# Feature sums taken from PSUM on VectorE, and split weights of the feed-forward part and of the attention's projections kept in DRAM

## The chip, the cores and the metric

The kernel runs on one core of a Trainium2 chip. The metric is the device time of one execution in microseconds (us). TensorE (PE) multiplies matrices, VectorE (DVE), ScalarE (ACT) and GpSimd (POOL) work on the elements, and SyncE (SP) issues most DMA transfers between DRAM and the on-chip memory SBUF. TensorE writes to a second memory, PSUM, which DVE and ACT read.

## The reference

A decoder layer on 1024 rows with 16 learned rows ahead of them, 1024 features, float32:

```python
u = rmsnorm(h, mix_norm_pre[l])
proj = u @ w_in[l]
q, f_logit, i_in, g_out, v_pool, gate_a, gate_b = jnp.split(proj, cuts, axis=-1)
a = hgrn2(q, f_logit, i_in, g_out, lbs[l], hgrn_out_norm[l])
p = multiscale_pool(v_pool, pool_proj[l], pool_scale[l])
z = (jax.nn.sigmoid(gate_a) * (a @ w_branch_hgrn[l])
     + jax.nn.sigmoid(gate_b) * (p @ w_branch_pool[l]))
h = h + rmsnorm(z @ w_out[l], mix_norm_post[l])
u = rmsnorm(h, ffn_norm_pre[l])
gt = causal_dwconv(u @ ffn_w_gate[l], ffn_conv_w[l], ffn_conv_b[l])
y = (jax.nn.gelu(gt, approximate=True) * (u @ ffn_w_up[l])) @ ffn_w_down[l]
h = h + rmsnorm(y, ffn_norm_post[l])
```

`hgrn2` is a gated linear recurrence over chunks of 64 rows (called the attention part below), `multiscale_pool` takes trailing means over 2, 4, 8 and 16 rows.

## The kernel before

**Precision.** Every operand of a large product is held as two tiles, `hi` (the value rounded to the reduced format fp32r) and `lo` (the rest). ACT makes `hi` with a cast, DVE or POOL makes `lo` with a subtraction; a product is hi x hi + hi x lo + lo x hi, three matmuls. Making the pair is called a split (`wsplit`, line 136 the cast, 137 the subtraction; for the products of the class `Strassen` lines 209 and 210).

**Stages, in order of time.** (1) 0 to about 70 us: the rows are normed, turned by TensorE (`feature_steps`: four transposes into a PSUM bank `pt`, from which ACT makes `uhi` and DVE `ulo`) and multiplied with the v columns of `w_in` (`v_mm`). The first weights are split by `split_wi` (line 447), in turn on DVE and POOL. (2) To about 100 us: two blocks of G (gate of the recurrence), loaded through a `Loader` that splits weights up to three blocks ahead. (3) To about 280 us: the gates a and b, as eight units of `Strassen`. (4) To about 500 us: the attention part, in the order written in `ORDER`: a capital name is a projection with a weight block of 1024 columns, `h0` to `h3` a step of a head. `POOLED` names operations that go to POOL, the splits `wF0`, `wQ0` and others among them. (5) To about 716 us: branch products, and the output projection in three chunks of rows; the rows of each chunk are normed and turned into features of the feed-forward part (`own.add`, `own.norm`, `own.feat`). (6) The feed-forward part: gate and up units of `Strassen` with the convolution on DVE and POOL beside them; then the down product.

**Strassen.** A unit is a product of 1024 x 256 weights with 1024 features x 1028 columns. It is cut into quarters and computed with seven products P1 to P7 in place of eight, each of four steps. Each needs a weight operand and a feature operand. P1, P2 and P4 take quarters of the weights, the others sums of them, which POOL makes (`load_unit`, lines 235 to 238: `swa`, `swb`). The feature operands are the quarters `b11`, `b21`, `b22` and the sums `t1` to `t4`. For the gates these sums are made by `gate_steps`, five generators of three steps each for five stretches of columns; the table `SUMS_AT` says after which tile which generator goes a step on. For the feed-forward part `to_quarters` makes them for each third of a chunk (114 rows, 456 columns in a tile of four feature blocks); the sums are shared between DVE (`combine`, lines 1061, 1063 and 1073) and POOL (`negdiff`, lines 1078 and 1079, and some `lo` tiles of line 334).

**The start of units.** The first `EARLY` = 4 units do P1 and P2 first, in pairs, since these need no sums: P1 goes to a PSUM pair, ACT copies it to SBUF (`p1s`), P2 goes to another pair, and DVE adds both into the result (`put_ffn`, line 1197), which frees the pair. `rest` does the other five. There are four PSUM pairs in this stage (pool `pf`), shared by products and the transposes' `pt` (line 1043). `ahead` splits weights up to four products ahead; on POOL for P1 and P2 of the second pair. Around the end of the output projection the order of PE, ACT, DVE and POOL is the order of the code (`manual_schedule`); each engine and the queue of SP work strictly in their own order.

**Buffers.** Weights rotate through three tiles each of `wraw` (raw), `whi` and `wlo`. `w_out`'s `lo` tiles are already kept in DRAM (`wlos`) by the first chunk for the other two.

```python
    def operand(self, u, p):
        if (u, "first") in self.raws and p in ("P1", "P2"):
            return self.raws[u, "first"][p == "P2"]
        if p in ("P1", "P2", "P4"):
            return self.raws[u, "raw"][("P1", "P2", "P4").index(p)]
        return self.sums[u][("P5", "P6", "P7", "P3").index(p)]
```

Of the kernel before, what the change touches and what calls it, by code (L numbers as in the profile page):

```python
# [14 lines left out]
P = 128  # L15
# [22 lines left out]
SUMS_AT = {5: (1,), 6: (1, 2), 7: (1, 2), 8: (3, 2), 9: (3, 4, 0), 10: (3, 4, 0), 11: (4, 0)}  # L38
# [18 lines left out]
def trunk_kernel(ctx: ExitStack, tc: tile.TileContext, x, meta_tokens, mix_norm_pre,  # L57
# [122 lines left out]
    class Strassen:  # L180
# [7 lines left out]
        def __init__(self, units, run, early, quarters, span, put, whole):  # L188
# [59 lines left out]
        def product(self, u, p, then=None):  # L248

            assert self.seq[self.at] == (u, p)  # L250
            x = pair(p)
# [4 lines left out]
            cuts = [(c0, o0, 512 - o0), (c0 + 512 - o0, 512, n - 512 + o0)][: 1 + (n + o0 > 512)]  # L256
            for k in range(4):
# [3 lines left out]
                for c, o, w in cuts:  # L261
                    pe.matmul(x[:, o : o + w], whi[:, k, :], xh[:, c : c + w], start=(k == 0), stop=False)  # L262
# [26 lines left out]
        def first(self, u):  # L289
# [3 lines left out]
            return (lambda: self.product(u, "P1", lambda x: act.copy(self.p1s[u], x)),  # L293
                    lambda: self.product(u, "P2", lambda x: self.put(u, 0, 0, self.p1s[u], x)))
# [1203 lines left out]
```

## Time and profile before

| | before |
|---|---|
| median of 3 runs | 1397.15 us (1396.82 to 1398.56) |
| the profiled execution | 1396.61 us |
| its span, first to last instruction | 1394.9 us |
| PE / DVE / ACT / POOL busy | 97% / 70% / 41% / 36% |
| mean granted clock of TensorE | 0.990 |
| read from and written to DRAM | 160.84 and 76.05 MB |

The profile shows one execution. L12 is line 12 of the kernel; `out<-in` are tiles by their names in the program, `[3.55 <-DVE wlo L137]` says that the engine stood idle for 3.55 us until DVE's instruction of line 137 had written `wlo`. "PEclk" is the share of the full clock that was granted to TensorE. About 1.7 us of the time lie outside the span.

### The profile page before, as it was taken

The numbers are of one execution on the slowest core, as the hardware profiler recorded it, in microseconds if no ns is written. First come the engines' busy times: TensorE is split into PE (matmuls) and PEld (weight loads), VectorE is DVE, ScalarE is ACT, GpSimd is POOL, SyncE is SP. The second block draws the span as 40 slices with busy tenths as digits, with TensorE's granted clock in tenths as the row PEclk, the third lists the DMA queues.
The fourth block names the chain that finished last, engine by engine and source line by source line (L and its number), as shares of the span: only waits on it lengthen the run. The fifth ranks groups of instructions, "written<-read, shape, count | busy, mean of one in ns | idle before, by whom it ended". The sixth has DMA issues, their size and how long they took to land. (4 is left out here: it accounts for less than half of the span.)

```text
span 1394.9 us, 21573 instructions
## 1 busy us (share of the span) xinstructions
PE 1353.6 (97%) x8405; PEld 1224.6 (88%) x8405; DVE 973.9 (70%) x1381; ACT 565.0 (41%) x945; POOL 508.4 (36%) x379
## 2 busy tenths in 40 slices
PE   8989999999999999999997999999999999999997
PEld 6879999999999899987777788888999988788786
DVE  6694655288975756565579888888887777654557
ACT  5443333356465463126564322222323223543343
POOL 4255331217543611051036565634567552000100
PEclk9999999999999999999998999999999999999999
DMA  6033433321111023589852577665677879966524
GB/s 245 31 100 121 138 104 108 103 73 46 33 33 33 18 76 122 182 265 316 288 172 91 148 218 214 192 173 145 161 166 188 197 194 268 365 231 201 179 71 166
DMA packets 133220, 215.21 MB, mean 154 GB/s; under 512 B 8327, under 2 KB 76523, under 8 KB 133120
## 3 DMA queue, kind: packets, MB, share of 16 engines
q1 hardware_dynamic: 121056, 189.47, 40.2%
q0 software_dynamic: 12064, 24.38, 10.3%
q8 instruction: 66, 1.08, 0.3%
q14 instruction: 34, 0.28, 0.1%
HBM read 160.84 MB, written 76.05 MB: 170 GB/s over the span
## 5 line engine op out<-in xcount | busy, mean ns | idle before, releaser
L262 PE MATMUL P<-v,whi 128*128 128x258 f32 (+2 forms) x528 | 162.6, 322 | 3.5 <-DVE g L1197 2.5
L263 PE MATMUL P<-v,whi 128*128 128x258 f32 (+2 forms) x528 | 161.6, 320 | 0.0
L265 PE MATMUL P<-v,wlo 128*128 128x258 f32 (+2 forms) x528 | 140.8, 321 | 1.1 <-DVE wlo L210 1.1
L137 POOL TENSOR_TENSOR wlo<-wraw,whi 128x1024 fp32r<-128x1024 f32 (+2 forms) x23 | 50.0, 2174 | 183.0 <-ACT whi L136 101.3
L262 PEld LDWEIGHTS P<-v,whi 128*128 128x128 f32 x528 | 100.8, 191 | 11.8 <-DVE g L1197 2.9
L263 PEld LDWEIGHTS P<-v,whi 128*128 128x128 f32 x528 | 100.7, 191 | 7.5
L161 PE MATMUL pd<-rot 128*128 128x512 f32 x272 | 106.0, 390 | 0.3 <-DVE rot L1257 0.3
L162 PE MATMUL pd<-rot 128*128 128x512 f32 x272 | 105.9, 389 | 0.0
L265 PEld LDWEIGHTS P<-v,wlo 128*128 128x128 f32 x528 | 87.9, 190 | 8.8 <-DVE wlo L210 1.3
L136 ACT CAST whi<-wraw 128x1024 fp32r<-128x1024 f32 (+2 forms) x44 | 36.2, 825 | 146.0 <-PE pba L174 31.3
L209 ACT CAST whi<-wraw 128x512 fp32r<-128x512 f32 x90 | 53.0, 617 | 101.8 <-PE P L263 83.9
L1257 DVE TENSOR_TENSOR rot<-yt,rot 128x1024 fp32r<-128x1024 f32 x33 | 41.2, 1250 | 71.0 <-ACT rot L1256 71.0
L210 DVE TENSOR_TENSOR wlo<-wraw,whi 128x512 fp32r<-128x512 f32 x82 | 75.9, 949 | 18.5 <-ACT whi L209 18.5
L1141 POOL TENSOR_TENSOR ys<-y 128x512 f32<-128x512 f32 x22 | 35.2, 1600 | 142.3 <-issue 96.8
L235 POOL TENSOR_TENSOR swa<-wraw,wraw 128x512 f32<-128x512 f32 x30 | 45.5, 1518 | 95.9 <-DMA wraw<-in_w_in_dram 62.4
L160 PE MATMUL pd<-rot 128*128 128x512 f32 x272 | 72.7, 390 | 2.0 <-ACT rot L1256 2.0
L1256 ACT CAST rot<-yt 128x1024 fp32r<-128x1024 f32 x33 | 34.6, 1053 | 90.2 <-PE pd L161 90.2
L209 ACT CAST whi<-swa 128x512 fp32r<-128x512 f32 x60 | 35.9, 619 | 86.8 <-PE P L263 71.6
L1189 DVE SCALAR_TENSOR_TENSOR y<-g,par,y 128x1024 f32<-128x1024 f32 x44 | 65.1, 1479 | 0.7
L160 PEld LDWEIGHTS pd<-rot 128*128 128x128 f32 x272 | 50.9, 188 | 13.5 <-ACT rot L1256 2.9
L210 DVE TENSOR_TENSOR wlo<-swb,whi 128x512 fp32r<-128x512 f32 x60 | 55.6, 932 | 9.7 <-ACT whi L209 9.4
L209 ACT CAST whi<-swb 128x512 fp32r<-128x512 f32 x60 | 35.9, 618 | 62.9 <-PE P L263 62.0
(344 smaller groups left out, 4320.2 us busy)
## 6 DMA issues: line engine op xcount, KB each, us to landing
wraw<-in_w_in_dram SPq DMA_DIRECT2D x36, 512.0 KB
yt<-ysum SPq DMA_DIRECT2D x33, 512.0 KB
wraw<-in_ffn_w_gate_dram SPq DMA_DIRECT2D x26, 512.0 KB
wraw<-in_w_out_dram SPq DMA_DIRECT2D x24, 512.0 KB
wraw<-in_ffn_w_up_dram SPq DMA_DIRECT2D x22, 512.0 KB
wsum<-in_ffn_w_down_dram SPq DMA_DIRECT2D x22, 512.0 KB
ysum<-ys SPq DMA_DIRECT2D x11, 768.0 KB
sa<-sscr SPq DMA_DIRECT2D x16, 513.0 KB
```

The costliest lines, as they stand in the source:

```text
L137: eng.tensor_tensor(lo, raw, rr(hi), ALU.subtract)
L160: pe.matmul(ps, ahi, bhi, start=first, stop=False)
L161: pe.matmul(ps, ahi, blo, start=False, stop=False)
L162: pe.matmul(ps, alo, bhi, start=False, stop=last)
L209: act.copy(hi, src)
L210: (pool_e if 4 <= i < 2 * self.early else dve).tensor_tensor(lo, src, rr(hi), ALU.subtract)
L235: pool_e.tensor_tensor(s1, a21, a22, ALU.add)
L262: pe.matmul(x[:, o : o + w], whi[:, k, :], xh[:, c : c + w], start=(k == 0), stop=False)
L263: pe.matmul(x[:, o : o + w], whi[:, k, :], xl[:, c : c + w], start=False, stop=False)
L265: pe.matmul(x[:, o : o + w], wlo[:, k, :], xh[:, c : c + w], start=False, stop=(k == 3))
L1189: dve.scalar_tensor_tensor(a, g[:, :, j : j + n], cvw[:, j, m : m + 1], a, ALU.mult, ALU.add)
L1257: dve.tensor_tensor(lo, src, rr(hi), ALU.subtract)
```

## The change

1. Ahead of everything else on TensorE stand five idle matmuls (`warm`) into a bank that nobody reads. All splits of `split_wi` are on DVE.
2. In `gate_steps` all of POOL's sums go to DVE. For the last three tiles t1 and t2 are made directly from the transposes' PSUM bank, right behind `ulo` (`more`). `SUMS_AT` is changed accordingly.
3. While the gates are computed, one job behind each half unit (`keep_next`): for the twelve weight blocks of F, Q and PV the split is made and `lo` written to DRAM (`keep_job`); for the first four feed-forward gate units P1's and P2's weights are split and both tiles written (`keep_first`). In the attention part F, Q and PV read `lo` back (`wload`), with no subtraction, and `ORDER` has seven new entries: `w4` (three) and `w5` (four), in each of which one or two weight operands of feed-forward units 0 (gate) and 4 (up) are summed on DVE, split and written to DRAM (`keep_unit`).
4. The first 20 products of the feed-forward part read both tiles from DRAM (`kept`), with no split and no sums. P2 of the first four units adds onto P1's PSUM pair (`onto`), after ACT has copied P1 out; ACT copies the result to the gate tile. The last chunk's feature sums are all on DVE, in pieces (`todo`) with a place of their own each.

```diff
-SUMS_AT = {5: (1,), 6: (1, 2), 7: (1, 2), 8: (3, 2), 9: (3, 4, 0), 10: (3, 4, 0), 11: (4, 0)}
+SUMS_AT = {5: (2,), 6: (2, 1), 8: (3,), 9: (1, 3), 10: (1, 4), 11: (4, 0), 12: (0, 0)}
...
+                if i % 2 == 0 and i // 2 < len(self.kept):
+                    parts_, tags = self.kept[i // 2]
+                    both = [wst.tile([P, 1024], F32R, tag=t, name=nm(t), bufs=NRAW) for t in tags]
+                    for t, src in zip(both, parts_):
+                        self.loaded = nc.sync.dma_start(rr(t), src)
...
-        def product(self, u, p, then=None):
+        def product(self, u, p, onto=None):
-            x = pair(p)
+            x = pair(p) if onto is None else onto
...
-        (pool_e if len(wi) % 2 else dve).tensor_tensor(lo, raw, rr(hi), ALU.subtract)
+        dve.tensor_tensor(lo, raw, rr(hi), ALU.subtract)
...
+    def sums_of(t0):
+        a = slice(t0 - 512, t0 - 512 + P)
+        t1, t2 = t12[a.start] = halves_tmp(P)
+        def more(j, src):
+            if j == 0:
+                dve.tensor_tensor(t1, src, rr(uhi[:, :4, a]), ALU.subtract)
+                dve.tensor_tensor(t1, t1, rr(ulo[:, :4, a]), ALU.subtract)
+            else:
+                dve.tensor_tensor(t2, src, t1, ALU.subtract)
+        return more
...
+    def keep_unit(u, w):
...
+        if u >= EARLY:
+            keep(((u, "P1"), a11), ((u, "P2"), a12))
+            yield
+        keep(((u, "P6"), ((a21, ADD, a22), (None, SUB, a11))), ((u, "P5"), ((a21, ADD, a22),)))
+        yield
+        keep(((u, "P3"), ((a21, ADD, a22), (None, SUB, a11), (a12, SUB, None))), ((u, "P7"), ((a11, SUB, a21),)))
+        yield
+        keep(((u, "P4"), a22))
...
+    def keep_job(kind, i):
+        raw = wraw_tile()
+        nc.sync.dma_start(raw.rearrange("p (k c) -> p k c", k=KD), job(kind, i)[0])
+        hi, lo = (wst.tile([P, 1024], F32R, tag=t, name=nm(t)) for t in ("whi", "wlo"))
+        act.copy(hi, raw)
+        dve.tensor_tensor(lo, raw, rr(hi), ALU.subtract)
+        kept_w[kind, i] = dram.tile([P, 1024], F32, name=f"kept{kind}{i}")
+        owed.append((kept_w[kind, i], rr(lo)))
+    def wload(*key):
...
+        nc.sync.dma_start(rr(lo), kept_w[key])
+        act.copy(hi, raw)
...
+        def first(e):
+            x[e] = ffn.product(e, "P1")
+            keep(e)
+        def second(e):
+            ffn.product(e, "P2", x[e])
+            act.copy(gate_tile(2 * UNITS[e][0])[:, 0], x[e][:, o : o + n])
```

The orders below give, for one engine, line, operation, output and inputs with their buffer numbers, and the tile.

DVE around the splits of G's weights (`L137`), before; `tt` are the gates' sums:

```order
L334 TENSOR_TENSOR t2l_578<-tt_121_638,t2h_576 128x2x128
L334 TENSOR_TENSOR t2l_579<-tt_121_638,t2h_577 128x2x128
L840 TENSOR_TENSOR tt_121_638<-tt_121_638,uhi_86 128x512
L842 TENSOR_TENSOR tt_121_638<-uhi_86,tt_121_638 128x512
L137 TENSOR_TENSOR wlo_721<-wraw_718,whi_720 128x1024
L137 TENSOR_TENSOR wlo_727<-wraw_724,whi_726 128x1024
```

The same place after the change; `L963` to `L967` are the first step of `gate_steps`, `L348` is the old line 334:

```order
L348 TENSOR_TENSOR t4l_628<-tt_64_355,t4h_626 128x2x128
L348 TENSOR_TENSOR t4l_629<-tt_64_355,t4h_627 128x2x128
L963 TENSOR_TENSOR tt_126_678<-ulo_87 128x512
L964 TENSOR_TENSOR tt_126_678<-uhi_86 128x512
L965 TENSOR_TENSOR tt_126_678<-tt_126_678 128x512
L966 TENSOR_TENSOR tt_126_678<-uhi_86,tt_126_678 128x512
L967 TENSOR_TENSOR tt_126_678<-tt_126_678,ulo_87 128x512
L137 TENSOR_TENSOR wlo_741<-wraw_738,whi_740 128x1024
L137 TENSOR_TENSOR wlo_747<-wraw_744,whi_746 128x1024
```

Ahead of the splits now stands the whole first step of one stretch, with the two operations that POOL did; the t1 and t2 of other stretches were made earlier.

DVE at the start of the feed-forward part, before: the last norm, the sum that frees P2's pair (`L1197`), the first third's sums (`tt_1041`, from the ACT copy `tt_1043`), the next release:

```order
L1120 SCALAR_TENSOR_TENSOR un_7222<-m_1008_7133,rstd_7226,g_790_6121 114x1024
L1197 TENSOR_TENSOR g_7254<-p_1015_7146,P_1031_7229 128x514
L1073 TENSOR_TENSOR tt_1041_7281<-tt_1043_7282,v_787_6117 128x456
L1073 TENSOR_TENSOR tt_1041_7281<-tt_1041_7281,v_787_6117 128x456
L1061 TENSOR_TENSOR tt_1041_7281<-tt_1043_7282,tt_1041_7281 128x456
L334 TENSOR_TENSOR t2l_6931<-tt_1041_7281,t2h_6929 128x2x114
L334 TENSOR_TENSOR t2l_6932<-tt_1041_7281,t2h_6930 128x2x114
L1063 TENSOR_TENSOR tt_1043_7282<-tt_1043_7282 128x456
L334 TENSOR_TENSOR v_788_6118<-tt_1041_7281,v_788_6118 128x4x114
L334 TENSOR_TENSOR t3l_6935<-tt_1043_7282,t3h_6933 128x2x114
L334 TENSOR_TENSOR t3l_6936<-tt_1043_7282,t3h_6934 128x2x114
L1197 TENSOR_TENSOR g_7328<-p_1015_7146,P_1044_7303 128x514
```

And after (`tt_1095` the first third's, `tt_1101` the second third's):

```order
L1262 SCALAR_TENSOR_TENSOR un_7455<-m_1074_7377,rstd_7459,g_857_6365 114x1024
L1215 TENSOR_TENSOR tt_1095_7471<-tt_1097_7472,v_854_6361 128x456
L1215 TENSOR_TENSOR tt_1095_7471<-tt_1095_7471,v_854_6361 128x456
L1202 TENSOR_TENSOR tt_1095_7471<-tt_1097_7472,tt_1095_7471 128x456
L348 TENSOR_TENSOR t2l_7175<-tt_1095_7471,t2h_7173 128x2x114
L348 TENSOR_TENSOR t2l_7176<-tt_1095_7471,t2h_7174 128x2x114
L1215 TENSOR_TENSOR tt_1101_7517<-tt_1103_7518,v_854_6361 128x456
L1215 TENSOR_TENSOR tt_1101_7517<-tt_1101_7517,v_854_6361 128x456
L1202 TENSOR_TENSOR tt_1101_7517<-tt_1103_7518,tt_1101_7517 128x456
L348 TENSOR_TENSOR t2l_7175<-tt_1101_7517,t2h_7173 128x2x114
L348 TENSOR_TENSOR t2l_7176<-tt_1101_7517,t2h_7174 128x2x114
```

No sum that frees a pair stands among them any more, t2 of the second third comes ahead of the first third's t1, t3 and t4, and those follow further down.

PE at the same place, before: the last two matmuls of P2 of unit 0, the transposes of the first third, P2 of unit 1:

```order
L265 MATMUL P_1031_7229<-v_787_6117,wlo_7139 128x258
L265 MATMUL P_1031_7229<-v_787_6117,wlo_7139 128x256
L1043 MATMUL pt_7272<-ident,un_7101 128x114 x8
L262 MATMUL P_1044_7303<-v_787_6117,whi_7138 128x258
L263 MATMUL P_1044_7303<-v_787_6117,whi_7138 128x258
```

And after: the last two of P1 of unit 1, the transposes, then P2 of unit 0, which goes to `P_1078`, the pair of its P1:

```order
L275 MATMUL P_1086_7424<-v_854_6361,wraw_7276 128x258
L275 MATMUL P_1086_7424<-v_854_6361,wraw_7276 128x256
L1182 MATMUL pt_7462<-ident,un_7341 128x114 x8
L272 MATMUL P_1078_7382<-v_854_6361,wraw_7336 128x258
L273 MATMUL P_1078_7382<-v_854_6361,wraw_7336 128x258
```

The transposes stand one product earlier, and fewer pairs are in use at once.

More of the change, by code (lines that the diff above doesn't have):

```diff
@@ L356, in norm_rows, with feature_steps @@
         return list(norm_steps(row, rows, gbc))[-1]
-    def feature_steps(un, rows, uhi, ulo, t_at):
+    def feature_steps(un, rows, uhi, ulo, t_at, more=None):
         for j in range(2):
@@ L434, in trunk_kernel, with warm @@
     g1 = slot(D, name="g1")
+    junk_bank = bank("pj")
+    def warm(n):
+        for _ in range(n):
+            pe.matmul(junk_bank[:, :P], onesm, ident, start=True, stop=True)
+    warm(2)
     gps = [bank("pg1") for _ in range(2)]
@@ new lines, in wload @@
+    def wload(*key):
+        raw = wraw_tile()
+        nc.sync.dma_start(raw.rearrange("p (k c) -> p k c", k=KD), job(*key)[0])
+        hi, lo = (wst.tile([P, 1024], F32R, tag=t, name=nm(t)) for t in ("whi", "wlo"))
+        nc.sync.dma_start(rr(lo), kept_w[key])
+        act.copy(hi, raw)
+        return tuple(t.rearrange("p (k c) -> p k c", k=KD) for t in (hi, lo))
+    beside = [lambda o=o_: keep_job(*o) for o_ in order if o_[0] in ("F", "Q", "PV")]
+    beside += [lambda e=e: keep_first(e) for e in range(EARLY)]
@@ L936, in trunk_kernel @@
     gates.finish()
+    pay()
     close_pool("pf")
     open_pool("ps", 8, PSUM)
-    loader = Loader([job(*o_)[:2] + (P, eng("w%s%d" % o_)) for o_ in order if o_[0].isupper()])
+    assert not beside
+    loader = Loader([o_ if o_ in kept_w else job(*o_)[:2] + (P, eng("w%s%d" % o_)) for o_ in order if o_[0].isupper()],
+                    lambda *a: wload(*a) if isinstance(a[0], str) else wsplit(*a))
     def split_z(c, k):
@@ L1273, in trunk_kernel @@
     last, t4s = None, []
+    assert ffn.seq[: len(KEPT)] == KEPT
+    ffn.kept = list(zip(kept, (("wraw", "wraw"), ("wraw", "wlo")) + (("whi", "wlo"),) * len(KEPT)))
     load_rows(0)
@@ L1295, in trunk_kernel @@
                             add_quarters("t2", "t3", "t4")
-                        t4s.append(last.feat(k - 2))
-                    if k > 4 and t4s:
-                        t4s.pop(0)()
+                        *now, late = last.feat(k - 2) or [None]
+                        for f in now:
+                            f()
+                        t4s += [late] * bool(now)
             if c < 2:
```

224 lines of the change are left out of this document (149 added, 75 removed).

## The prediction

> **What bounds the kernel now.** I read the page's busy times first, then the busy times by stretches, then what TensorE waited for.
>
> ```profile
> span 1394.9 us, 21573 instructions
> PE 1353.6 (97%) x8405; PEld 1224.6 (88%) x8405; DVE 973.9 (70%) x1381; ACT 565.0 (41%) x945; POOL 508.4 (36%) x379
> ```
>
> TensorE is busy for 1353.6 of 1394.9 us. The change leaves its number of products as it is, so it can only win back some of the 41.3 us in which TensorE stands still, and the time in which it runs at half its clock. The table by stretches says where these lie. Its columns are the stretch, its length, then busy time (instructions) of PE, PEld, DVE, ACT and POOL, then the granted clock, the DMA share and GB/s.
>
> ```profile
> 20.00:60.00 40.00, 40.00 (x205) 33.16 (x204) 24.51 (x47) 20.46 (x43) 3.57 (x4) 1.00 0.24 78
> 60.00:80.00 20.00, 16.42 (x69) 13.82 (x68) 19.69 (x21) 8.92 (x20) 14.01 (x9) 0.84 0.17 52
> 100.00:120.00 20.00, 17.63 (x148) 17.64 (x149) 4.90 (x15) 8.55 (x22) 11.56 (x11) 1.00 0.33 111
> 130.00:280.00 150.00, 150.00 (x1225) 150.00 (x1225) 74.12 (x98) 50.18 (x85) 41.51 (x28) 1.00 0.36 116
> 340.00:480.00 140.00, 136.18 (x1052) 132.28 (x1051) 112.23 (x234) 76.40 (x122) 67.14 (x31) 0.99 0.11 31
> 640.00:700.00 60.00, 57.70 (x271) 44.05 (x270) 33.53 (x50) 37.05 (x70) 0.00 (x0) 1.00 0.88 306
> 700.00:716.00 16.00, 15.15 (x69) 11.08 (x68) 13.64 (x25) 10.65 (x29) 6.49 (x8) 1.00 0.47 158
> 700.00:720.00 20.00, 18.09 (x91) 13.78 (x90) 17.57 (x31) 14.31 (x37) 6.49 (x8) 1.00 0.45 150
> 720.00:740.00 20.00, 16.68 (x141) 16.25 (x139) 16.95 (x18) 10.02 (x23) 10.78 (x8) 0.98 0.49 152
> 740.00:760.00 20.00, 13.84 (x78) 13.43 (x79) 18.87 (x25) 10.23 (x25) 11.60 (x9) 0.67 0.24 79
> 760.00:780.00 20.00, 18.29 (x115) 15.82 (x114) 17.04 (x18) 6.82 (x13) 18.52 (x18) 1.00 0.35 80
> 780.00:800.00 20.00, 18.25 (x105) 15.84 (x105) 18.50 (x24) 6.11 (x10) 6.29 (x6) 1.00 0.62 182
> ...
> 72.00:82.00 10.00, 6.49 (x27) 6.49 (x28) 9.83 (x9) 3.76 (x9) 7.79 (x5) 0.66 0.44 134
> 740.00:750.00 10.00, 6.39 (x32) 6.39 (x33) 9.41 (x13) 3.41 (x10) 6.96 (x6) 0.52 0.47 157
> 756.00:760.00 4.00, 3.91 (x18) 3.72 (x19) 3.98 (x6) 3.92 (x10) 2.71 (x2) 0.57 0.00 0
> ```
>
> ```profile
> PE pt L1043 <- DVE g L1197: 6.2, 1, 6.2
> PE pg L177 <- DVE wlo L137: 3.6, 1, 3.6
> PE P L262 <- ACT sg L714: 2.7, 1, 2.7
> PE P L262 <- ACT t2h L333: 2.5, 1, 2.5
> ```
>
> These are TensorE's waits (total, times, longest). The five stretches from 700 to 800 us hold 100 - (18.09 + 16.68 + 13.84 + 18.29 + 18.25) = 14.85 us of idle TensorE. A stall also slows what follows: at 740 to 750 us the clock is 0.52, so 6.39 us busy are worth 3.3 and 3.1 are lost; at 756 to 760 us another 3.91 x 0.43 = 1.7. The start of the feed-forward part thus costs 14.85 + 3.1 + 1.7 = 19.6 us, and only 0.85 of it (idle from 700 to 716) belongs to the output projection. The wait for G's weights costs 3.55 us plus 6.49 x 0.34 = 2.2 of lost clock.
>
> **Part 1, the first microseconds.** A row of the groups by line (gates, 130 to 280 us) gives the price of a split of 1024 columns on DVE with little beside it; then rows in order of time (start, duration).
>
> ```profile
> L137 DVE TENSOR_TENSOR wlo<-wraw,whi 128x1024 fp32r<-128x1024 f32 x1 | 1.2, 1226 | 0.2 <-ACT whi L136 0.2
> ...
> 2.44 3.75 PE L437 MATMUL pg<-g1row,ones 1*128 1x512 f32 x4 [2.44 <-DMA g1row<-in_mix_norm_pre_dram]
> 6.62 0.86 DVE L352 SCALAR_TENSOR_TENSOR un<-row,rstd,g 128x512 f32<-128x512 f32 x1
> 7.63 1.09 PE L363 MATMUL pt<-ident,un 128*128 128x128 f32 x4 [1.45 <-POOL mask L495]
> 11.35 3.56 DVE L352 SCALAR_TENSOR_TENSOR un<-row,rstd,g 128x512 f32<-128x512 f32 x2
> 11.70 2.66 POOL L447 TENSOR_TENSOR wlo<-wiraw,whi 128x1024 fp32r<-128x1024 f32 x1 [2.73 <-ACT whi L446]
> 12.08 0.63 PE L160 MATMUL pv<-whi,uhi 128*128 128x512 f32 x1
> ...
> 12.51 0.63 PE L161 MATMUL pv<-wlo,uhi 128*128 128x512 f32 x1
> ...
> 16.04 0.39 PE L161 MATMUL pv<-wlo,uhi 128*128 128x512 f32 x1
> ...
> 16.27 0.39 PE L162 MATMUL pv<-whi,ulo 128*128 128x512 f32 x1
> ```
>
> The two halves of the second norm take 3.56 us beside POOL's weight split; alone one took 0.86, so 1.8 us of stretching goes. In its place DVE has the split to do, 1.23 us, which may come before or after them. I take -1. The first six products start 0.43 us apart (12.08, 12.51) and from 16.04 on 0.23: at full pace they would save 6 x 0.2 = 1.2 us if nothing else held them. Bounds: 0 and -2. The five idle matmuls go ahead of the gain's broadcast, which waits for its DMA until 2.44. Five at the 0.27 us of a transpose are 1.4 us, twice that if each is two passes. The gain is broadcast until 6.19 and its second half copied only after the first norm half (7.48), so about 1.2 us of delay is covered besides the wait for the DMA: cost 0 (at most 0.6). The Trainium skill ("TensorE: Matmul & The Clock Gate", Part 1) holds that the clock is released only after about 3.4 us of sustained work, in free-running windows; by that the idle matmuls, a gap of over 1 us behind them, wake nothing early and the term is -1; were they to wake it, -2. The stretch from 12 to 16 us fits the rule, but says nothing on so short a burst.
>
> **Part 2, the gates' sums and G's weights.**
>
> ```profile
> 71.85 0.68 DVE L840 TENSOR_TENSOR tt<-tt,uhi 128x512 f32<-128x512 f32 x1
> 73.17 4.50 DVE L137 TENSOR_TENSOR wlo<-wraw,whi 128x1024 fp32r<-128x1024 f32 x2
> 75.51 0.94 PE L177 MATMUL pg<-uhi,wlo 128*128 128x342 f32 x2 [3.55 <-DVE wlo L137]
> ```
>
> DVE is busy for 19.69 of the 20 us from 60 to 80. The first split of G's weights starts at 73.17, behind the sums L840 and L842, and two splits take 4.50 us beside POOL's sums where one alone takes 1.23. After the change nothing of POOL's stands beside them, and three tiles' first sums (three operations of 0.68 each, 6.1 us) are made earlier, between the v products, where DVE is busy for 24.51 of 40 us and TensorE for all (20 to 60). Against this the second halves of POOL's sums come to DVE: about two more operations per tile, 1.4 us, and five sums now stand straight ahead of the splits. The splits themselves end 2 us sooner than 4.50, and the queue ahead of them is shorter by the contention of five to ten operations. I take the stall as gone with its lost clock, 3.55 + 2.2, but for 0.3: -5.5. Bounds: 0 (the queue is as late as before) and -5.8. What is late next is the wait of 2.7 us for the change of PSUM pools (L714), which stays.
>
> **Part 3, the weights kept in DRAM.** While the gates are computed, 12 jobs each split 1024 columns and four split two halves of 512: on DVE 12 x 1.23 + 8 x 0.68 = 20 us, on ACT about as much. From 130 to 280 us DVE is busy for 74.12 of 150 us and ACT for 50.18, TensorE for all 150.00: the cover is there. DMA moves 12 x 1 MB + 4 x 1.5 MB more, 120 GB/s on top of 116, and 306 GB/s have been seen (640 to 700). I take +1; with 0.3 us lost at each of 16 jobs it would be +5, and 0 is the other end.
>
> In the attention part the splits of F, Q and PV leave POOL (ten) and DVE (two), and their place is taken by seven pieces w4 and w5, 26 DVE operations of 512 columns, 26 x 0.68 = 17.7 us.
>
> ```profile
> 352.66 3.40 POOL L137 TENSOR_TENSOR wlo<-wraw,whi 128x1024 fp32r<-128x1024 f32 x1
> 353.72 3.44 DVE L626 TENSOR_TENSOR kd<-kd,kk 128x1040 f32<-128x1040 f32 x1
> ```
>
> The DVE operation of 1040 columns took 3.44 us beside POOL's split, 1.23 being the price of 1024 alone. At 1 to 2 us each the ten POOL splits have cost DVE 10 to 20 us, the two DVE splits at least 2.5: relief and new work come out near each other. DVE is busy for 112.23 of the 140 us, and the stretch has 3.8 us of idle TensorE. I take +1, bounds -4 (all that idle) and +6 (a third of the new work uncovered).
>
> **Part 4, the start of the feed-forward part.**
>
> ```profile
> 736.96 1.69 DVE L1063 TENSOR_TENSOR tt<-tt 128x456 f32<-128x456 f32 x1
> ...
> 743.61 1.78 PE L1043 MATMUL pt<-ident,un 114*128 114x114 f32 x8 [6.20 <-DVE g L1197]
> ...
> 747.15 0.70 DVE L334 TENSOR_TENSOR t2l<-tt,t2h 128x228 fp32r<-128x228 f32 x2 [0.45 <-ACT t2h L333]
> 747.77 0.63 DVE L1063 TENSOR_TENSOR tt<-tt 128x456 f32<-128x456 f32 x1
> ```
>
> The wait of 6.20 us: the transposes need the PSUM pair that the gate sum L1197 frees, and this stands on DVE behind the whole of the first third's sums, each slowed by POOL (1.69 us against 0.63 for L1063). After the change P2 is added onto P1's pair and ACT copies it out, so that no release stands behind DVE's sums; the splits of these products and POOL's sums of units 0 and 4 are gone. What DVE then has is eight operations of 456 columns and three pairs of 228 for each third: 3 x (8 x 0.63 + 3 x 0.70) = 21.4 us. TensorE's first eight products are 24 matmuls each, of 0.12 us by the gates (1225 matmuls in 150.00 us), 2.9 us a product, and with the three thirds' transposes (at most 1.5 us each, by the 743.61 row and the next product at half clock) 25 to 27 us. It fits, but in places only just. I went through the new order by hand with these durations. TensorE waits 1.1 us before P2 of unit 2 and 2.45 before P2 of unit 3 (ACT's copy of P1 stands behind casts that wait for DVE), 0.95 before P6 for the last third's t2, and 1.95 in four later places: 6.5 us in place of 19.6 - 0.85 = 18.8, a gain of 12.3. Waits of 2.5 (t2h) and 2.7 us (sg) stand in the list above; behind the first the clock fell to 0.57 and 1.7 us went, behind the second it stayed at 1.00 (100 to 120 us). So I charge 1 us for the wait of 2.45 and take -11. Bounds: -5, if each of those waits is twice as long, and -17, if hardly any comes. The Trainium skill (same page and part) puts the fall of the clock at an idle window of about 3.4 us. By that a wait of 2.45 us would cost no clock, the term would be -12 and the time 1380, inside the forecast's own range; the row at 756 to 760 us speaks against the rule as an exact threshold.
>
> The kept operands, 20 halves of 512 KB or 10.5 MB, have to come within some 60 us, 175 GB/s, where half of that came as raw weights before (150 GB/s from 700 to 740) and 306 were seen: hidden, and if not, the gain of this part shrinks by the same time.
>
> **Sum.** -1 - 5.5 + 1 + 1 - 11 = -15.5. The profiled execution took 1396.61 us, 0.54 under the median of 1397.15: 1396.6 - 15.5 = 1381.1.
>
> **Rivals.**
> - The sums stay the bound at the feed-forward start (DVE busy 17 to 19 of 20 us there speaks for it; that POOL's share is slowing it speaks against): -5 for -11, 1387.
> - All goes better: -17 there, -4 in the attention part, 0 in the gates, 1396.6 - 1 - 5.8 - 4 - 17 = 1369. Against it: the hand reckoning leaves waits.
> - It does not do what it says: DVE reaches G's weights as late as before and the kept operands come so late that TensorE waits as long as it did: terms 0 and 0, 1396.6 - 1 + 1 + 1 = 1397.6. Against it stands the DMA rate above.
> - Slower: the pieces w4 and w5 come where DVE has no room (340 to 480 us), and TensorE waits for all of their 17.7 us, with one more fall of the clock (2.2): +20 in place of +1, 1396.6 - 1 - 5.5 + 1 + 20 - 11 = 1400. It decides once more than 16.5 us of the 17.7 and its after-effects are uncovered. Against it: 27.8 us of free DVE in that stretch, and what POOL's splits no longer cost.
>
> **How the numbers follow.** Forecast (1376 to 1385) 0.53, sums stay the bound 0.20, better 0.12, no effect 0.07, slower 0.08. The range from 1368 to 1394 leaves out the last two and the end of the better case, and takes in the bounds of parts 2 and 4 one at a time (forecast with part 2 at 0: 1386.6; with part 4 at -5: 1387; both, 1392.6). A measurement of this kernel tells about 0.2%, 2.8 us, from no change: faster 0.85, same 0.07, slower 0.08.
>
> **What would show it.** In the profile after: no wait of pg for wlo near 72 us and a clock of 1.00 from 72 to 82; no wait of pt for L1197's successor; TensorE busy over 93 of the 100 us behind the output projection's end, with its waits naming ACT's p1 copies and t2; 150 us of full TensorE in the gates as before; idle time in the attention part near 3.8 us. The forecast is wrong if idle time there grows beyond 10 us, or if products wait for DMA of the kept tiles.

## The result and the profile after

The changed kernel takes 1387.03 us (median of 4 runs, 1386.05 to 1390.67) against 1397.86 of the kernel before beside it: a ratio of 0.9927, interval 0.991 to 0.9945. That is faster by 0.7%, inside the range and above the forecast's own 1376 to 1385. The page's busy times after:

```profile
span 1386.2 us, 21763 instructions
PE 1352.8 (98%) x8415; PEld 1224.7 (88%) x8415; DVE 970.8 (70%) x1436; ACT 578.4 (42%) x961; POOL 419.7 (30%) x320
```

TensorE's work is the same; of the 8.7 us that the span lost, 7.9 are idle time of TensorE. The stages show that this is a difference of large terms. Lengths in us, read from the order in time of each profile, each from the first matmul of a stage to the first of the next (start to the first gate product; gates to the first F product; attention to the first branch product; branch products; output projection). The feed-forward units count to the start of their last matmul, and the down product from there to the start of its own last:

| kernel | start, v, G | gates | attention | branch | output proj. | feed-forward | down |
|---|---|---|---|---|---|---|---|
| before | 102.4 | 160.0 | 250.4 | 94.2 | 109.2 | 458.0 | 213.3 |
| after | 93.8 | 168.0 | 260.0 | 94.8 | 108.4 | 440.3 | 213.2 |
| difference | -8.6 | +8.0 | +9.6 | +0.6 | -0.8 | -17.7 | -0.1 |

Busy times by these stretches, gates, attention and feed-forward units, before (columns as in the prediction):

```profile
102.37:262.35 159.98, 159.98 (x1345) 159.98 (x1346) 78.39 (x106) 54.87 (x95) 54.34 (x38) 1.00 0.36 118
262.35:512.78 250.43, 246.61 (x1837) 240.58 (x1836) 186.90 (x383) 136.63 (x219) 108.93 (x52) 0.99 0.14 42
716.14:1174.16 458.02, 444.01 (x2796) 401.54 (x2795) 383.10 (x455) 143.67 (x247) 254.76 (x194) 0.99 0.67 179
```

and after:

```profile
93.79:261.77 167.98, 162.55 (x1344) 161.96 (x1345) 97.35 (x135) 70.52 (x121) 52.41 (x37) 0.99 0.68 213
261.77:521.76 259.99, 249.55 (x1836) 242.28 (x1835) 196.13 (x407) 144.81 (x233) 89.62 (x43) 0.99 0.32 105
724.92:1165.23 440.31, 438.01 (x2796) 397.29 (x2795) 364.56 (x451) 135.64 (x233) 220.88 (x167) 1.00 0.73 199
```

In the gates TensorE stood still for nothing before and for 5.4 us now, and in the attention part for 10.4 us in place of 3.8, though DVE is busy for only 97 of 168 and 196 of 260 us. In the feed-forward units its idle time fell from 14.0 to 2.3 us. TensorE's longest waits after follow; the wait for G's weights is gone from the list:

```profile
PE ppp L173 <- DVE sc L697: 3.6, 1, 3.6
PE P L272 <- ACT whi L217: 2.8, 1, 2.8
PE P L272 <- ACT p L1473: 1.8, 2, 1.2
PE pj L456 <- POOL ident masks.py:199: 1.6, 1, 1.6
```

**The gates.** Rows in order of time around the wait of 2.8 us for `whi`:

```profile
152.21 0.38 SPq L236 DMA_DIRECT2D wraw<-in_w_in_dram  x1
...
156.75 1.30 POOL L243 TENSOR_TENSOR swa<-wraw,wraw 128x512 f32<-128x512 f32 x1 [11.30 <-DMA wraw<-in_w_in_dram]
...
159.26 1.72 POOL L244 TENSOR_TENSOR swa<-swa,wraw 128x512 f32<-128x512 f32 x1
...
160.98 1.04 ACT L924 CAST whi<-wraw 128x1024 fp32r<-128x1024 f32 x1 [1.74 <-DMA wraw<-in_w_in_dram]
...
161.93 0.61 ACT L217 CAST whi<-swa 128x512 fp32r<-128x512 f32 x1
```

and the second raw load of the same unit (the fourth) before, where the gates start 8.6 us later:

```profile
142.27 0.42 SPq L228 DMA_DIRECT2D wraw<-in_w_in_dram  x1
```

The unit's second raw half is asked for 58.4 us after the gates' first product (152.21 - 93.79) where it was 39.9 before (142.27 - 102.37): its buffer had just been released by a kept job's subtraction (L925). POOL waits for it, its sums are late, and on ACT the cast of the next kept job (L924) stands ahead of the one that TensorE needs, itself waiting for a load. The stall also took clock (0.72):

```profile
162.00:168.00 6.00, 5.40 (x32) 5.40 (x33) 4.29 (x6) 3.26 (x7) 0.33 (x1) 0.72 0.94 270
```

The rest of the 5.4 us are two stalls of 1.3 and 1.4 us, up to 211.45 and 215.93 us. Ahead of the first, a cast on ACT had waited 2.58 us for a raw load; ahead of the second, a subtraction on DVE had waited 3.02 us for the store of a job's `lo`. Between the stalls, with the jobs running, TensorE is never idle:

```profile
118.00:159.50 41.50, 41.50 (x350) 41.50 (x349) 22.91 (x31) 14.63 (x23) 9.89 (x8) 1.00 0.68 210
168.00:209.50 41.50, 41.50 (x350) 41.50 (x349) 27.08 (x33) 18.12 (x28) 12.38 (x8) 1.00 0.75 231
217.00:261.70 44.70, 44.70 (x378) 44.70 (x377) 28.43 (x40) 20.35 (x34) 7.01 (x5) 1.00 0.81 259
```

**The attention part.** DVE and POOL ahead of the wait of 3.6 us (TensorE's last matmul before it starts at 469.62; the kernel before had one of 2.5 us near this place, up to 477.06, so 1.1 us of it are new):

```profile
466.01 2.41 DVE L871 TENSOR_TENSOR wlo<-wlo,wraw 128x512 f32<-128x512 f32 x1
...
467.95 4.56 POOL L776 TENSOR_TENSOR s<-s 128x1037 f32<-128x1037 f32 x2
...
468.74 2.00 DVE L871 TENSOR_TENSOR wlo<-wraw,wlo 128x512 f32<-128x512 f32 x1
...
470.66 2.39 DVE L874 TENSOR_TENSOR wlo<-wlo,whi 128x512 fp32r<-128x512 f32 x1
...
472.98 1.28 DVE L697 COPY_PREDICATED sc<-mbase,sb 128x128 f32<-128x128 uint8 x6
```

L871 and L874 are a piece w5. The copies L697, which free the PSUM banks that the next projection needs, stand behind them, and each operation takes 2.0 to 2.4 us beside POOL's sums instead of 0.68. The Trainium skill ("SBUF — State Buffer", Who interferes with whom) states that a DVE instruction with two inputs in SBUF contends with a GpSimd instruction that reads SBUF; these rows agree.

More of the new idle time lies elsewhere. From 363 to 379 us there are four waits of 0.9 to 1.4 us, 4.3 us in all, among the operations of a piece w4 on DVE (L871 and L874); the kernel before has no wait over 0.7 us there. And at the start of the stage, up to 266.45 us, TensorE waits 1.2 and 1.1 us for the first casts of `wload` (L934).

### The profile page after: what moved, and what is told of

Its sections match the earlier page's. It is cut to its first block, busy times and chain, and to the rows that moved or that the text cites. A ratio compares the mean times of both kernels' runs of the same rounds, so it can differ in the third digit from the quotient of the medians.

```text
span 1386.2 us, 21763 instructions
## 1 busy us (share of the span) xinstructions
PE 1352.8 (98%) x8415; PEld 1224.7 (88%) x8415; DVE 970.8 (70%) x1436; ACT 578.4 (42%) x961; POOL 419.7 (30%) x320
## 5 line engine op out<-in xcount | busy, mean ns | idle before, releaser
L272 PE MATMUL P<-v,whi 128*128 128x258 f32 (+1 forms) x496 | 153.4, 323 | 2.3 <-ACT p L1473 1.8
L273 PE MATMUL P<-v,whi 128*128 128x258 f32 (+1 forms) x496 | 152.3, 321 | 0.0
L275 PE MATMUL P<-v,wlo 128*128 128x256 f32 (+2 forms) x512 | 136.7, 320 | 0.0
L272 PEld LDWEIGHTS P<-v,whi 128*128 128x128 f32 x496 | 93.5, 189 | 10.3 <-ACT p L1473 2.2
L273 PEld LDWEIGHTS P<-v,whi 128*128 128x128 f32 x496 | 93.7, 189 | 7.6
L275 PEld LDWEIGHTS P<-v,wlo 128*128 128x128 f32 x512 | 84.8, 189 | 7.8
L217 ACT CAST whi<-wraw 128x512 fp32r<-128x512 f32 x78 | 46.2, 617 | 95.8 <-PE P L273 79.2
L243 POOL TENSOR_TENSOR swa<-wraw,wraw 128x512 f32<-128x512 f32 x28 | 42.5, 1519 | 117.4 <-DMA wraw<-in_w_in_dram 73.5
L217 ACT CAST whi<-swa 128x512 fp32r<-128x512 f32 x56 | 33.5, 618 | 94.2 <-PE P L273 64.6
L160 PEld LDWEIGHTS pd<-rot 128*128 128x128 f32 x272 | 51.0, 188 | 13.4 <-ACT rot L1399 1.6
L218 DVE TENSOR_TENSOR wlo<-swa,whi 128x512 fp32r<-128x512 f32 x56 | 51.7, 932 | 15.4 <-ACT whi L217 10.4
L161 PEld LDWEIGHTS pd<-rot 128*128 128x128 f32 x272 | 51.1, 188 | 11.3 <-DVE rot L1400 0.7
L162 PEld LDWEIGHTS pd<-rot 128*128 128x128 f32 x272 | 51.1, 188 | 10.6
L272 PE MATMUL P<-t2h,whi 128*128 128x258 f32 (+1 forms) x196 | 57.1, 308 | 2.8 <-ACT whi L217 2.8
```

What stands on the lines that cost most here:

```text
L160: pe.matmul(ps, ahi, bhi, start=first, stop=False)
L161: pe.matmul(ps, ahi, blo, start=False, stop=False)
L162: pe.matmul(ps, alo, bhi, start=False, stop=last)
L217: act.copy(hi, src)
L218: (pool_e if 4 <= i < 2 * self.early else dve).tensor_tensor(lo, src, rr(hi), ALU.subtract)
L243: pool_e.tensor_tensor(s1, a21, a22, ALU.add)
```

## Experiments

Stage lengths of all runs, in us, with the time and the ratio to the kernel before. The lengths are those of one profiled execution each. In the seven runs whose feed-forward part is that of the changed kernel, that column goes from 440.3 to 444.2, so a difference of 3 or 4 us there says little:

| run | gates | attention | branch | output proj. | feed-forward | median | ratio (interval) |
|---|---|---|---|---|---|---|---|
| after | 168.0 | 260.0 | 94.8 | 108.4 | 440.3 | 1387.03 | 0.9927 (0.991 to 0.9945) |
| e_sums | 160.2 | 250.7 | 94.4 | 108.7 | 458.9 | 1388.91 | 0.9947 (0.993 to 0.9964) |
| e_nojobs | 168.2 | 259.1 | 94.9 | 109.3 | 441.1 | 1388.57 | 0.9938 (0.9918 to 0.9958) |
| e_ownraw | 181.6 | 265.2 | 94.9 | 109.9 | 443.9 | 1405.67 | 1.0061 (1.0043 to 1.0078) |
| e_late | 168.4 | 251.9 | 94.2 | 108.6 | 440.4 | 1379.89 | 0.9878 (0.9857 to 0.9899) |
| e_lateall | 160.3 | 250.7 | 106.5 | 114.1 | 444.2 | 1387.70 | 0.9932 (0.991 to 0.9953) |
| e_actstore | 176.1 | 267.4 | 94.8 | 108.7 | 443.4 | 1403.83 | 1.005 (1.0033 to 1.0067) |
| e_nounits | 167.7 | 254.6 | 94.2 | 108.7 | 455.1 | 1394.62 | 0.9987 (0.9975 to 0.9999) |
| e_pool | 168.2 | 261.6 | 94.8 | 108.9 | 440.1 | 1390.94 | 0.9966 (0.9946 to 0.9986) |
| e_late_own3 | 168.7 | 252.9 | 94.8 | 109.2 | 441.8 | 1382.52 | 0.9894 (0.9876 to 0.9911) |
| e_unitsonly | 160.3 | 250.7 | 94.4 | 108.1 | 445.9 | 1375.12 | 0.985 (0.9831 to 0.987) |
| e_jobdma | 160.3 | 250.7 | 95.2 | 108.7 | 446.6 | 1376.21 | 0.9829 (0.9809 to 0.9849) |
| e_jobwork | 160.3 | 250.6 | 95.5 | 108.7 | 447.2 | 1377.55 | 0.9838 (0.9815 to 0.9861) |

**e_sums: part 2 (and the first splits) alone.** The kernel before with:

```diff
+SUMS_AT = {5: (2,), 6: (2, 1), 8: (3,), 9: (1, 3), 10: (1, 4), 11: (4, 0), 12: (0, 0)}
-        pool_e.tensor_tensor(t2, b12l, b11l, ALU.subtract)
+        dve.tensor_tensor(t2, b12l, b11l, ALU.subtract)
...
-        (pool_e if len(wi) % 2 else dve).tensor_tensor(lo, raw, rr(hi), ALU.subtract)
+        dve.tensor_tensor(lo, raw, rr(hi), ALU.subtract)
```

> The kernel before with part 2 and the first weights' splits on DVE alone: nothing is kept in DRAM, no idle matmuls, the feed-forward part as before. Theory: the whole gain between 60 and 102 us comes from this part, so the first gate product starts at about 93.8 us as in the changed kernel (102.4 before), all later stages keep their lengths, and the time is 8 to 9 us under before (ratio about 0.994). Rival: part of that gain needs the rest of the change (fewer POOL operations later, other buffer use); then the first gate product starts later than 97 us and the gain is under 5.5 us.

The first gate product starts at 93.49 us, and all later stages have their old lengths. The gain up to the gates is this part's alone: the theory holds. Alone it makes the kernel 8.0 us faster (1396.91 to 1388.91), where the whole change gains 10.8: parts 3 and 4, which make up most of the code, add some 3 us to it.

**e_nojobs: without the twelve jobs for F, Q and PV.**

```diff
-    beside = [lambda o=o_: keep_job(*o) for o_ in order if o_[0] in ("F", "Q", "PV")]
-    beside += [lambda e=e: keep_first(e) for e in range(EARLY)]
+    beside = [lambda e=e: keep_first(e) for e in range(EARLY)]
```

> The changed kernel without the twelve jobs for F, Q and PV: their splits are made in the attention part on POOL and DVE as before; the four jobs for the first feed-forward products and w4, w5 stay. Theory (the twelve jobs cost the gates 8 us, w4 and w5 cost the attention part its 10): gates 160 to 163 us instead of 168, attention part (first F product to first branch product) 260 us or some more, since POOL's splits come back beside w4 and w5: time 1379 to 1386. Rival (reading lo back and ACT's casts at the head of its queue cost the attention part, not w4 and w5): attention part 250 to 253 us, time 1369 to 1373.

The gates stay at 168.2: my price by the number of jobs fell. Four jobs at the worst place cost as much as sixteen. The rows at the one long stall:

```profile
152.58 1.29 DVE L874 TENSOR_TENSOR wlo<-wraw,whi 128x512 fp32r<-128x512 f32 x2 [3.10 <-DMA kept3l<-wlo]
...
153.90 0.38 SPq L236 DMA_DIRECT2D wraw<-in_w_in_dram  x1
...
159.81 1.26 POOL L243 TENSOR_TENSOR swa<-wraw,wraw 128x512 f32<-128x512 f32 x1 [13.89 <-DMA wraw<-in_w_in_dram]
...
161.10 0.62 ACT L217 CAST whi<-swa 128x512 fp32r<-128x512 f32 x1 [9.36 <-POOL swa L243]
```

The chain is that of the changed kernel: a raw buffer that a job's subtraction (L874, itself behind a wait for an earlier store) frees late, the raw load 60.9 us after the gates' start, POOL's sum, the cast. The stall is 4.9 us long, and the clock behind it is 0.50 from 165 to 168 us and 0.78 to 171. From 165 us on, with no jobs, TensorE is busy all the time. The attention part, which here reads no `lo` back but still has w4 and w5, falls by only 0.9 us, so the theory is right there: the pieces cost 8 to 9 us. The waits at the start of that stage are gone in this run; they come with the reading back.

**e_ownraw: the jobs' raw tiles from another pool.**

```diff
-        raw = wraw_tile()
+        raw = slot(1024, name="kraw")
```

> The changed kernel, but the jobs beside the gates take their raw weights into a buffer of the feature pool, so the three raw buffers serve the gates' units alone. Theory (the gates' 8 us come from the raw buffers' rotation: the next unit's weights are loaded late): gates 160 to 162 us instead of 168, time 1379 to 1382. Rival (the jobs' work on DVE and ACT or their DMA delays the gates): gates 166 to 169 us, time 1385 to 1389.

Slower by 0.6%: the raw buffers alone are not the cause. The gates' products now end 170.3 us after their start, and a wait of 11.1 us follows. What SP waited for from 90 to 280 us in this run says where the jobs pass the wait on (L817 and L819 are the gates' own stores, which wait long without any job, too: 86 us in the kernel before):

```profile
SPq L819 <- ACT sg L815: 42.1, 14, 7.5
SPq L888 <- DVE wlo L925: 25.6, 12, 6.0
SPq L817 <- ACT sg L815: 21.5, 13, 5.3
SPq L888 <- ACT whi L873: 16.5, 5, 4.9
```

The jobs' stores (L888) wait at the head of SP's queue for tiles that are late, with the units' loads behind them.

**e_late: w4 and w5 among the branch products.**

```diff
-F2 w4 h1 c2 h0 Q2 w4 h1 h2 G2 w4 ... F3 w5 ... PV0 w5 ... PV1 w5 ... PV2 w5 ... BB1 BB2 sa2 BB3 h3 BB4
+F2 h1 c2 h0 Q2 h1 h2 G2 ... F3 ... PV0 ... PV1 ... PV2 ... BB1 w4 BB2 sa2 w4 BB3 h3 w4 BB4
-BB5 sa0 sa3 BA0 BA1 BB6 BA2 BB7 BA3 BA4
+BB5 sa0 sa3 w5 BA0 BA1 w5 BB6 BA2 w5 BB7 BA3 w5 BA4
```

> The changed kernel with the seven pieces w4 and w5 moved out of the attention part, to between the branch products BB1 and BA4, where DVE is busy for 80 of 140 us. Theory (the attention part's 10 us are DVE's 26 operations of these pieces ahead of copies that free PSUM): first F product to first branch product 250 to 253 us instead of 260, the branch products 0 to 3 us longer, time 1377 to 1382. Rival (the loads of lo and ACT's casts cost it): that stretch stays at 258 to 261, time 1385 to 1390.

Attention 251.9, branch products 94.2, as the theory has it, and a kernel faster than the one before and the changed one. The same 26 DVE operations cost nothing there, as the row of the branch products shows (DVE 63.54 of 94.17 us, TensorE all of them):

```profile
512.19:606.36 94.17, 94.17 (x592) 92.99 (x591) 63.54 (x102) 35.44 (x53) 13.50 (x9) 1.00 0.71 246
```

**e_lateall: all of the keeping among the branch products.** No jobs for F, Q and PV; `keep_first` there as well, as k0 to k3. Against e_late's order:

```diff
-BB0 h2 ... BB4 BB5 ... BB7 BA3 w5 BA4 BA5
+BB0 k0 h2 ... BB4 k1 BB5 ... BB7 k2 BA3 w5 BA4 k3 BA5
```

> Nothing is kept during the gates and the attention part: no jobs for F, Q and PV (split on POOL and DVE as before), and the four jobs for the first feed-forward products as well as w4 and w5 stand among the branch products BB0 to BA5. Theory (the gates' 8 us and the attention part's 10 are the price of keeping, where it was put): gates 160 to 161 us, first F product to first branch product 250 to 251, branch products 94 to 99 instead of 95, feed-forward part as in the changed kernel: time 1368 to 1375. Rival (the jobs only meet another limit there: DMA or the raw buffers): branch products and output projection 8 us or more longer, time over 1377.

Gates and attention are back at 160.3 and 250.7, but the branch products take 12 us more and the output projection 5: the rival came true. What TensorE waited for longest in that run:

```profile
PE pba L173 <- ACT whi L136: 5.0, 3, 2.5
```

The branch products' own weights now come late: from 500 to 700 us ACT waits 16.1 us, in five waits, for loads of them. On SP's queue the kept stores wait 23.9 us for casts in that time; how much of the delay is theirs, and how much that of the DMA rate (261 GB/s in the branch products, 167 in the changed kernel), is open.

**e_actstore: the jobs' stores on ACT's queue.**

```diff
-        pay()
         if beside:
             beside.pop(0)()
+        pay(nc.scalar)
```

> The changed kernel, but the jobs' stores beside the gates are issued on ACT's queue right behind each job, not on SP's ahead of the next loads. Theory A (SP works in order, and the stores, waiting for DVE's lo and standing behind the gates' own stores, hold up the next unit's loads): gates 160 to 164 us instead of 168, time 1379 to 1384. Theory B (the buffers shared with the jobs set when the loads can start, whatever the queue): gates 166 to 170, time 1385 to 1390.

176.1 us, worse than either theory said. Where ACT has to wait for DVE before it can issue the store, everything behind it waits too. ACT's longest wait from 90 to 270 us (9.9 us in the changed kernel, to 262 us):

```profile
ACT whi L217 <- DVE wlo L925: 21.8, 10, 5.2
```

On SP's part in the loss this run says nothing.

**e_nounits: only the first eight products kept.**

```diff
-    KEPT += [(0, p) for p in Strassen.ORDER[2:]] + [(UP0, p) for p in Strassen.ORDER]
...
         second(0)
+        ffn.load_unit(RUN[0])
         do(0)
...
+        ffn.load_unit(RUN[1])
         ffn.rest(RUN[0], dict(P6=[lambda: do(2, 3)]))
```

> The changed kernel with only the first eight feed-forward products kept; the rest of unit 0 and unit 4 are loaded raw, summed on POOL and split on DVE as before, and w4, w5 are gone. Theory: the attention part is short again (first F product to first branch product 250 to 253), and the feed-forward part's products take 443 to 449 us instead of 440, so half or more of its 18 us come from the first eight products, the PSUM release and the sums' place: time 1380 to 1387. Rival (the kept units 0 and 4 carry that gain): 450 to 458 us, time 1388 to 1396.

The attention part falls to 254.6 with w4 and w5 gone, though not to 250 to 253. What is left lies at its start: TensorE waits 2.7 us for the first casts of `wload`, and the clock falls to 0.61 and 0.53 (264 to 272 us). e_late waits 2.1 us there, with 0.62 and 0.96. So the reading back costs some 1.5 to 4 us. In the feed-forward part the rival came true: 455.1 us, so the kept units 0 and 4 carry 14.8 of the 17.7 us when they are taken away alone. The rows around one of three long waits (3.3, 3.0 and 3.4 us) show how:

```profile
736.77 1.44 POOL L246 TENSOR_TENSOR swb<-wraw,swa 128x512 f32<-128x512 f32 x1
...
736.98 2.38 DVE L1214 TENSOR_TENSOR tt<-tt,v 128x456 f32<-128x456 f32 x2
...
740.14 0.67 ACT L347 CAST t2h<-tt 128x228 fp32r<-128x228 f32 x2 [3.80 <-DVE tt L1201]
...
742.28 0.39 PE L272 MATMUL P<-v,whi 128*128 128x258 f32 x1 [3.26 <-ACT p L1472]
```

Unit 0's weight sums are back on POOL beside DVE's feature sums (1.19 us each against 0.63); ACT's copy of P1 stands behind the cast that waits for them, and P2, which goes to the same pair, waits 3.26 us for the copy.

**e_pool: the last chunk's feature sums shared with POOL again.**

```diff
-        todo.append(own.feat(0, dve))
+        todo.append(own.feat(0))
```

(the same for 1 and 2)

> The changed kernel with the last chunk's b22, t4 and difference sums back on POOL, all else as changed. Theory (POOL's operations beside DVE's stretch DVE's chain): feed-forward products 443 to 450 us instead of 440, time 1390 to 1397. Rival (the gain is that no release of PSUM stands behind the sums; who makes them matters little): 439 to 442 us, time 1386 to 1389.

The stage took 440.1 us in the profiled execution (1388.11 us), as in the changed kernel: who makes these sums mattered nothing there, as the rival has it. But the ten times of this kernel go from 1386.45 to 1397.90, and their median of 1390.94 lies in the theory's range; the ratio's interval lies just above the changed kernel's. The times of 1396 and more have a mean clock of 0.985 to 0.987, the profiled one 0.993. What they lost, and in which stage, was not profiled, so the question is open.

**e_late_own3: e_late with buffers of their own for raw, hi and lo of the jobs.**

```diff
-        raw = wraw_tile()
+        raw = slot(1024, name="kraw")
...
-        hi, lo = (wst.tile([P, 1024], F32R, tag=t, name=nm(t)) for t in ("whi", "wlo"))
+        hi, lo = (slot(1024, F32R, t) for t in ("khi", "klo"))
```

> As the run with w4 and w5 among the branch products, and besides the jobs beside the gates have buffers of the feature pool for raw, hi and lo alike; stores and loads stay on SP. Theory (what the jobs share with the gates' units is the rotation of all three kinds of buffers, and the order of SP's queue only passes that wait on): gates 160 to 164 us instead of 168, time 1371 to 1376. Rival (any 16 loads and stores in SP's in-order queue between the gates' own loads and stores cost it, whatever buffers they use): gates 166 to 175 us, time 1379 to 1388.

Gates 168.7: the rival's length, so it is not the buffers alone. What ACT waited for from 90 to 260 us:

```profile
ACT khi L924 <- DMA kraw<-in_w_in_dram: 35.4, 12, 7.3
ACT sg L815 <- DVE sg L812: 19.9, 15, 3.2
```

With the buffers free, each of the twelve jobs' casts reached the head of ACT's queue before its load had landed, and ACT stood there for 35.4 us in all.

**e_unitsonly: no job beside the gates, only units 0 and 4 kept, w4 and w5 late.**

```diff
+    beside = []
...
-    ffn.kept = list(zip(kept, (("wraw", "wraw"), ("wraw", "wlo")) + (("whi", "wlo"),) * len(KEPT)))
+    ffn.kept = [None] * 4 + [(k_, ("whi", "wlo")) for k_ in kept[4:]]
...
-        ffn.ahead(2)
+        ffn.load_first(0)
+        ffn.load_first(1)
+        ffn.load_first(2)
```

> As the run with w4 and w5 among the branch products, but without any job beside the gates: F, Q and PV are split in the attention part as before, and the first eight feed-forward products are loaded raw and split as before, on POOL for four of them; only units 0 and 4 are kept. Theory (the gates' 8 us are the jobs', and the kept units carry most of the feed-forward part's 18 us): gates 160 to 161, first F product to first branch product 250 to 252, feed-forward products 441 to 448 instead of 440, time 1372 to 1379. Rival (without the first eight kept the feed-forward start stalls as before): feed-forward products 450 us or more, time over 1381.

All as the theory had it, at 1375.12 us the fastest median of these runs, 1.5% under the kernel before. Against e_late, keeping the first eight products is worth 445.9 - 440.4 = 5.5 us in the feed-forward part, with the scatter of that stage between 2 and 7, and its jobs cost the gates 8 (e_nojobs has no others).

**e_jobdma and e_jobwork: the jobs' two halves.** Both add 16 jobs to e_unitsonly, at the same places and with buffers of their own; nothing reads their results:

```diff
+    def keep_beside(src, n):
+        raw = slot(1024, name="kraw")
+        nc.sync.dma_start(raw.rearrange("p (k c) -> p k c", k=KD), src)
+        for i in range(n):
+            owed.append((spare[i], raw))
```

```diff
+    def keep_beside(src, n):
+        hi, lo = (slot(1024, F32R, t) for t in ("khi", "klo"))
+        for i in range(n):
+            c = slice(i * 1024 // n, (i + 1) * 1024 // n)
+            raw = rr(uhi[:, 0, c])
+            act.copy(hi[:, c], raw)
+            dve.tensor_tensor(lo[:, c], raw, rr(hi[:, c]), ALU.subtract)
```

> As the run that keeps units 0 and 4 alone, with 16 jobs beside the gates that only move data: each loads 512 KB into a buffer of its own and stores it to a spare place in DRAM (four of them twice), all on SP's queue, with no cast and no subtraction; nothing reads what they store. Theory A (the jobs' transfers in SP's queue hold up the gates' own loads and stores): gates 165 us or more instead of 160, time 1379 to 1385. Theory B (the jobs' casts and subtractions at the head of ACT's and DVE's queues do it): gates 160 to 162, time 1374 to 1377.

> As the run that keeps units 0 and 4 alone, with 16 jobs beside the gates that only work: the same casts on ACT and subtractions on DVE, from a tile that lies in SBUF, into buffers of their own; no loads, no stores, and nothing reads the results. Theory A (SP's queue): gates 160 to 162 us, time 1374 to 1377. Theory B (ACT's and DVE's queues): gates 165 us or more, time 1379 to 1385. If both this run and the one with transfers alone stay at 160 to 162, it is the two together: casts that wait for their loads at the head of ACT's queue, and stores that wait for the casts at the head of SP's.

The gates of e_jobdma, then of e_jobwork:

```profile
92.12:252.41 160.29, 160.29 (x1345) 160.29 (x1345) 77.22 (x115) 56.36 (x103) 52.95 (x38) 1.00 0.70 225
```

```profile
93.11:253.40 160.29, 160.29 (x1344) 160.29 (x1345) 95.92 (x133) 70.71 (x121) 58.36 (x38) 1.00 0.36 118
```

TensorE is busy for all 160.29 us in both. The transfers alone (225 GB/s, as many bytes as in the changed kernel) cost nothing, and the work alone (DVE 96, ACT 71 us, as much as there) costs nothing. Both side by side, untied, were not run; but in the changed kernel both go on side by side in the stretches between the stalls (the three lines under "The gates", up to 259 GB/s), and TensorE is busy for all of these. The 8 us are the price of the two tied together: a cast that waits for its load at the head of ACT's queue, and loads and stores in SP's that wait for buffers and results. The two links shown are the late raw load in the changed kernel and in e_nojobs and ACT's waits in e_late_own3; how the 8 us divide between them is open. Jobs whose cast stands one job behind their load, in buffers of their own, were not tried.

## Why the prediction was right, and where it was off

1. **The first microseconds** (-1): right in size on average, but not in the profile of the result, where it is +0.2. In the twelve profiles with this part and the idle matmuls the last v product starts at 68.6 to 70.5 us, 69.3 on average, against 70.33 before. The idle matmuls took 2.50 us from 1.60 on and moved the gain's broadcast from 2.44 to 4.04. They woke nothing early: the first six products still start 0.4 to 0.8 us apart, as before. What the kernel would take without them was not tried.
2. **The gates' sums** (-5.5): -8.6 up to the gates. The stall at 72 us went with its clock, as reckoned. The step that failed is that the wait of 2.7 us for L714 would stay. It was the same cause: ahead of the sigmoid that frees the banks ACT had casts that waited for POOL's sums (before),

```profile
99.34 0.71 ACT L333 CAST t3h<-tt 128x256 fp32r<-128x256 f32 x2 [4.88 <-POOL tt L841]
...
101.87 1.14 ACT L714 ACTIVATE sg<-pg 128x342 f32<-128x342 f32 x3
```

and with these sums done earlier TensorE's wait there is 0.23 us. 3.55 + 2.2 + 2.4 = 8.2, near the 8.6 us by which the two blocks of G got shorter (31.6 to 23.0).
3. **Keeping beside the gates** (+1, at most +5): +8.0, outside its bounds. "The cover is there" was read from busy time, DVE's 74 of 150 us. e_jobwork shows that this was true of the work, and e_jobdma of the transfers; the step left out was that each job chains a load, a cast, a subtraction and a store through queues and buffers on which the units' own loads depend. The price went with the chain at its worst place, not with the number of jobs, 16 times 0.3.
4. **Keeping in the attention part** (+1, at most +6): +9.6. The slower rival had the mechanism, w4 and w5 where DVE has no room, at twice its size (+20). e_late shows it: the same pieces elsewhere give 8.1 us back, with the branch products unchanged. The rest is the reading back of `lo` at the start of the stage, for which the prediction had no term. The relief from POOL's ten splits did not balance them, since what counted was which copies stood behind the pieces, not DVE's sum of busy time.
5. **The feed-forward start** (-11, at most -17): -17.7, all of it in the first 20 products. Right in mechanism, too small in size: of the 6.5 us of waits reckoned by hand 2.3 came, and the clock held at 1.00. The reason given for the contention was in part wrong: the feature sums on POOL cost nothing in the one profile of e_pool (its median leaves it open), but POOL's weight sums and the splits of units 0 and 4 did (e_nounits). No run takes the adding of P2 onto P1's pair away alone, so its own share is open.

In the profile the five terms come to -8.5 in place of -15.5: two costs were under-reckoned by 16 us, two gains by 10, and the first term came 1 short. The range held because these cancel in part, which is luck. The measured 1387.03 is the time of the first rival, too (the sums stay the bound, 1387), but not by its mechanism: the feed-forward start gained more than reckoned, not less.

Of the signs that the prediction named, those of parts 2 and 4 came: no wait for G's `wlo` near 72 us, a clock of 1.00 from 72 to 82 us, and TensorE busy for 97.7 of the first 100 us of the feed-forward units. Those of part 3 did not: TensorE is busy for 142.2 of the 150 us from 130 to 280, and stands still for 10.4 us in the attention part. The prediction calls itself wrong if that goes beyond 10 us. By this sign its part 3 was wrong, though the time is in the range.

On the clock: the stall of 2.8 us up to 162.60 was followed by 0.72 from 162 to 168 us, while the stalls of 1.3 and 1.4 us up to 211.45 and 215.93 left it at 1.00. The Trainium skill ("TensorE: Matmul & The Clock Gate", Part 1) gives an idle window of about 3.4 us. Here shorter ones were enough in three places: that of 2.8 us, and in the kernel before two of 2.5 us, up to 477.06 (0.76 from 478 to 482 us) and up to 756.04 (0.57 from 756 to 760). The 2.7 us up to 102.37 there left it at 1.00. So the charge that the prediction made for a wait of 2.45 us was reasonable; that wait did not come (the longest was 1.2 us), and nothing here shows what it would have cost.

## What to carry to other kernels

Idle shares of engines say whether extra work fits, not whether it can be placed: ask for each added load, cast and store what stands behind it in its in-order queue and which shared buffer it holds until when. Where TensorE waits for PSUM, look at what stands ahead of the releasing copy on its engine, before looking at how fast that engine is. A change that gains in one stage and pays in two others is best taken apart by stage lengths: here a part of it, in another place (e_unitsonly), gave a gain of 22 us in place of 11.

## What was not expected of the hardware

A job of transfers alone at 225 GB/s and a job of work alone at 0.6 of DVE's and 0.44 of ACT's time each left TensorE busy for 160.29 of 160.29 us, while both chained cost 8 us with a lower total load on DMA (213 GB/s). Four jobs (e_nojobs) cost as much as sixteen, by one stall of 5 us and the lower clock behind it.
